# Value, key and query projections with 512 weight columns per matmul instead of 256

## The chip, the cores and the metric

The kernel runs on one core of a Trainium2 chip. The metric is the device time of one execution in microseconds, as a median of three runs. Engines are called as the profile calls them: PE is TensorE (matmuls), PEld its weight loads, DVE is VectorE, ACT is ScalarE, POOL is GpSimd and SP is the queue from which most transfers are issued.

## The reference

One layer of a diffusion backbone for 1024 latent tokens and 256 context tokens, width 1024, in float32. In order: a SwiGLU feed-forward half step (hidden width 2816), a mixer with two branches, and a second SwiGLU half step, each normalized and modulated by values that come from a conditioning vector. The change concerns the mixer, where one projection gives the inputs of both branches:

```
hx = modulate(rms_norm(x, norm2_g), ml[3], ml[4])
hc = modulate(rms_norm(cx, norm2_g), mc[3], mc[4])
bg_l, cg_l, vc_l, q_l, k_l, v_l, gt_l = split(hx @ w_in)      # widths 1024 x3, q 1024, k 256, v 256, 2048
..., k_c, v_c, ... = split(hc @ w_in)
y_conv_l = bg_l * short_conv(cg_l * vc_l, conv_w)
q_l, k_l, v_l = split_heads(q_l, k_l, v_l, q_norm_g, k_norm_g)  # RMS norm of each head of q and k
q_l, k_l = axial rotary of q_l and k_l                          # latent tokens alone
o_l = attention(q_l, [k_c, k_l], [v_c, v_l])                    # 8 query heads, 2 key/value heads of 128
x = x + ml[5] * merge_branches(y_conv_l, o_l, gt_l, ...)
```

Only the latent stream is returned.

## The kernel before

Each float32 operand of a product is split into a high part that a matmul takes exactly (float32r) and a low part, the rest. A product is then three matmuls (`mm3`): high by high, high by low, low by high. Splitting a tensor (`split`) is a cast on ACT for the high part and a subtraction on DVE for the low part.

The kernel goes through these stages: the first feed-forward net, the mixer's wide projections (a form of Strassen's products, the class `Winograd`, object `mix`), then v, k and q, then the convolution's output product, attention, the merge, and the second feed-forward net. Convolution products and attention are interleaved.

**v.** `load_256` fetches 256 columns of `w_in` as two pieces of 1024 elements on each partition (`load_w`: one transfer into a `raw` tile, a high part in a `wh` tile, a low part in a `wl` tile). `proj_256` makes the product for 128 tokens: the tokens' normalized values (`h_hi`, `h_lo`; 8 tiles of 128 rows of the contraction) are the stationary side, 256 weight columns the moving side, 8 x 3 matmuls into half a PSUM bank. The v loop does so for 2 context and 8 latent token tiles; after each, `split` puts the result into v's high and low tiles.

**k and q.** `heads2` is a generator in three steps for two heads and one chunk of tokens (`CC`: 256 context tokens, `C0` and `C1`: 512 latent tokens each). Step one: for each pair of token tiles four times 128 columns into one bank, a copy by ACT (`xb`), four squares with sums by ACT (`hsq`). Step two: eleven small DVE instructions for the reciprocal root (`rsqrt_cols`), a scaling of each head and token tile by DVE, and for latent tokens the rotary: POOL multiplies the swapped halves (`hsw`), DVE the rest, DVE adds. Step three: PE transposes, and the result is copied (q) or split (k). There are 3 such units for k and 8 for q (four pairs of heads by two chunks). The loop at the end of the stage runs a unit's first step, then the last step of the unit before, so that PE has products while DVE works on the former.

**Queues and pools.** The order that is written is not the order on the engines. When the program is built, a planner with its own estimates of durations sets each engine's order: it takes what is ready and stands earliest in the program; `pinned=True` ties an instruction behind the one traced before it on its engine. Tiles of a tag share a fixed number of slots, and a new tile waits until a slot's last reader is done: 3 `raw`, 4 `wh`, 4 `wl` (also used by `mix` and, for `wl`, by the convolution's weights), 38 large tiles of 1024 elements, 11 of 512 elements, 5 PSUM banks for products, 2 for transposes. Transfers of one queue are issued in their planned order.

**Beside the stage.** `late_steps` is the modulation for the second feed-forward net: four halves of 19 steps, 8 of which are a multiply-add of 512 columns on DVE (`macc`). Three steps are run after each v tile, five after each unit of heads. `mix.part_second` splits the first half of `C1`'s normalized values, which `mix` itself needs unsplit. `conv_weights` and `conv_inputs` fetch and split what the convolution product needs.

## Time and profile before

| what | value |
|---|---|
| median of three runs | 2670.65 us (2669.2 to 2675.72) |
| the profiled execution | 2670.08 us |
| its span, first to last instruction | 2668.3 us |
| busy PE, weight loads, DVE, ACT, POOL | 99%, 83%, 75%, 44%, 21% |
| granted TensorE clock | 0.996 |
| first v product to the last q product | 1287.23 to about 1446.3 us |

Line numbers are all L90, because every engine call goes through one helper; instructions are told apart by the tiles that they write and read. In a row such as `ps<-wh,r`, `ps` is a PSUM bank, `wh` a weight tile and `r` the normalized tokens; `h2ch` and `h2cl` are the context tokens' parts. A timeline's row has the start in the span, the length and, behind `x`, how many like instructions were joined; the brackets show how long the engine had sat idle and what it waited for. Matmuls overlap, so a matmul's own length (0.28 us for 256 columns, 0.39 for 512) says little of their pace.

### The profile page before, as it was taken

What the parts mean: (1) busy time and instruction counts of PE and PEld (TensorE: products, weight loads), DVE (VectorE), ACT (ScalarE), POOL (GpSimd) and SP (SyncE); (2) the same over time, 40 slices, a digit from 0 to 9 for tenths busy, and PEclk for the clock granted to TensorE, in tenths of its full rate; (3) what the DMA queues carried; (4) which work ended last, traced back from release to release, by engine and by line L of the source; (5) the groups of instructions that cost most, each with busy time, mean ns of one, the idle gap of its engine ahead of it and who ended that gap; (6) DMA issues with size and microseconds to landing.
All of it is one profiled execution on the core that took longest, in us unless ns stands there. A gap on an engine that the chain in (4) does not pass through costs nothing.

```text
span 2668.3 us, 36840 instructions
## 1 busy us (share of the span) xinstructions
PE 2633.8 (99%) x13373; PEld 2220.0 (83%) x13373; DVE 2002.0 (75%) x3356; ACT 1173.6 (44%) x2317; POOL 558.4 (21%) x449
## 2 busy tenths in 40 slices
PE   8999999999999999999999999999999999999998
PEld 6787799888778878888999888888888888888888
DVE  5788976788887899877598676685458976657885
ACT  6532454333454643333355576574236333334443
POOL 0134301111020034332033122141001532330200
PEclk9999999999999999999999999999999999999999
DMA  8566475345984355342522432113525643227841
GB/s 320 194 194 189 138 230 158 115 131 187 302 206 119 126 179 173 98 134 72 202 68 92 91 95 62 35 41 98 167 87 171 196 146 97 86 88 285 188 90 64
DMA packets 371471, 381.12 MB, mean 143 GB/s; under 512 B 19526, under 2 KB 258264, under 8 KB 371288
## 3 DMA queue, kind: packets, MB, share of 16 engines
q1 hardware_dynamic: 360472, 357.22, 41.4%
q0 software_dynamic: 10816, 21.53, 4.9%
q8 instruction: 105, 1.72, 0.3%
q14 instruction: 78, 0.64, 0.1%
HBM read 308.88 MB, written 69.76 MB: 142 GB/s over the span
## 4 chain that ended last, share of the span: by engine, by line
PE 90%; DVE 5%; DMA 2%; issue 1%; ACT 1%; POOL 1%; SPq 0%; DVEq 0%; POOLq 0%; ACTq 0%
PE ps L90 74%; PE po L90 8%; PE pt L90 8%; DVE wl L90 1%; DVE r L90 1%; DMA raw<-in_ffn_w_in_dram 1%; DVE nt L90 0%; DMA rawm<-in_w_mod_dram 0%; DMA ws<-in_ffn_w_out_dram 0%; DVE u L90 0%; DVE macc L90 0%; POOL s L90 0%; DVE y L90 0%; POOL sum L90 0%; DVE sq_acc L90 0%
## 5 line engine op out<-in xcount | busy, mean ns | idle before, releaser
L90 PE MATMUL ps<-r,wl 128*128 128x512 f32 x5196 | 1206.8, 391 | 9.6 <-DVE wl L90 3.1
L90 PEld LDWEIGHTS ps<-r,wl 128*128 128x128 f32 x5196 | 974.4, 189 | 218.8 <-DVE wl L90 5.9
L90 ACT CAST wl<-raw 128x512 fp32r<-128x512 f32 x287 | 177.7, 620 | 229.8 <-PE ps L90 173.3
L90 DVE TENSOR_TENSOR wl<-raw,wl 128x512 fp32r<-128x512 f32 x287 | 202.3, 706 | 60.6 <-ACT wl L90 56.7
L90 ACT CAST wl<-sum 128x512 fp32r<-128x512 f32 x168 | 103.2, 620 | 231.9 <-PE ps L90 184.9
L90 DVE TENSOR_TENSOR wl<-sum,wl 128x512 fp32r<-128x512 f32 x168 | 152.2, 908 | 17.8 <-ACT wl L90 16.8
L90 POOL TENSOR_TENSOR sum<-raw 128x512 f32<-128x512 f32 x42 | 60.6, 1443 | 497.9 <-DMA raw<-in_w_in_dram 203.2
L90 DVE SCALAR_TENSOR_TENSOR macc<-rawm,silu_c,macc 128x512 f32<-128x512 f32 x178 | 148.0, 849 | 13.5 <-DMA rawm<-in_w_mod_dram 12.8
L90 DVE TENSOR_TENSOR u<-u,ps 128x512 f32<-128x512 f32 x186 | 126.2, 680 | 33.6 <-PE ps L90 33.6
L90 PE MATMUL ps<-wh,r 128*128 128x256 f32 x768 | 141.6, 284 | 0.0
L90 DVE TENSOR_TENSOR pts<-pt,pts 128x512 fp32r<-128x512 f32 x160 | 108.7, 687 | 41.1 <-ACT pts L90 39.3
L90 ACT CAST pts<-pt 128x512 fp32r<-128x512 f32 x160 | 93.3, 595 | 86.4 <-PE pt L90 82.7
L90 DVE TENSOR_REDUCE m<-ps 128x1 f32<-128x512 f32 (+1 forms) x192 | 110.3, 595 | 23.9 <-PE ps L90 22.3
L90 ACT CAST rh<-hid 128x512 fp32r<-128x512 f32 x132 | 81.3, 620 | 104.6 <-PE ps L90 91.6
L90 PE MATMUL ps<-rh,wl 128*128 128x512 f32 x360 | 122.0, 389 | 0.0
L90 PEld LDWEIGHTS ps<-wh,r 128*128 128x128 f32 x768 | 120.8, 192 | 0.7 <-issue 0.6
L90 POOL TENSOR_TENSOR sum<-raw,sum 128x512 f32<-128x512 f32 x42 | 62.0, 1476 | 268.7 <-DVE wl L90 261.8
L90 ACT CAST wh<-raw 128x512 fp32r<-128x512 f32 (+1 forms) x85 | 67.9, 801 | 103.2 <-PE ps L90 70.2
L90 POOL TENSOR_TENSOR s<-raw 128x512 f32<-128x512 f32 x22 | 32.0, 1457 | 378.5 <-DMA raw<-in_ffn_w_in_dram 297.1
L90 PE MATMUL po<-pts,vh 128*128 128x512 f32 x256 | 110.0, 435 | 0.2 <-ACT pts L90 0.2
L90 PE MATMUL ps<-wl,r 128*128 128x256 f32 x384 | 109.0, 284 | 0.0
L90 DVE TENSOR_TENSOR rl<-hid,rh 128x512 fp32r<-128x512 f32 x132 | 90.3, 686 | 21.7 <-PE ps L90 11.7
(317 smaller groups left out, 5382.9 us busy)
## 6 DMA issues: line engine op xcount, KB each, us to landing
raw<-in_ffn_w_in_dram SPq DMA_DIRECT2D x130, 512.0 KB
raw<-in_ffn_w_out_dram SPq DMA_DIRECT2D x72, 512.0 KB
raw<-in_w_in_dram SPq DMA_DIRECT2D x61, 512.0 KB
rawm<-in_w_mod_dram SPq DMA_DIRECT2D x104, 256.0 KB
hid<-hd SPq DMA_DIRECT2D x40, 512.0 KB
rawm<-in_w_mod_dram SPq DMA_DIRECT2D x32, 512.0 KB
ws<-in_ffn_w_out_dram POOLq DMA_DIRECT2D x30, 512.0 KB, 6.5
ucd<-uc SPq DMA_DIRECT2D x29, 512.0 KB
```

The source lines that it names most:

```text
L90: inst = getattr(self.engine, name)(*args, **kw)
```

## The change

One product now makes 512 columns. k and v lie side by side in `w_in`, so k's two heads and v share a product; q is made four heads at a time. `load_512` fetches 512 columns as four pieces, each with 256 rows of the contraction. `tokens2` takes the place of `heads2` and of the v loop, with the same three steps, for two token tiles and `n_h` heads (2 with v, 4 for q): 1 + 4 units for k and v, 2 x 4 for q, 13 in all. Each token tile has a bank of its own; in the last unit of each group (`at_once`) the two banks are filled side by side, piece by piece. `part_second` moves from before v to behind the first unit, nine late steps are run after each unit, the rotary products are written one token tile at a time, and the convolution's first weights are fetched behind the last unit's products instead of before them.

```diff
-    for k in range(4):
-        mix.part_second(k)
...
-    def load_256(o):
+    def load_512(o):
         return [
-            load_w(wi[h * 512 : (h + 1) * 512, o : o + 256].rearrange("(k p) n -> p k n", p=P), (4, 256))
-            for h in range(2)
+            load_w(wi[i * 256 : (i + 1) * 256, o : o + 512].rearrange("(k p) n -> p k n", p=P), (2, 512))
+            for i in range(4)
         ]
...
-    vw = load_256(O_V)
+    kv_w = load_512(O_K)
...
-    for kt in range(10):
-        ch = CC if kt < 2 else C0 if kt < 6 else C1
-        o = (kt if kt < 2 else (kt - 2) % 4) * P
-        pv_ = ps_s(256)
-        proj_256(pv_, vw, ch, o)
-        split(pv_, *v_tile(kt))
-        run(late_steps, 3)
...
+    def tokens2(w, ch, b, n_h, g, dst, values=None, at_once=False):
+        s, o, _ = ch
+        banks, ts = [ps_s(), ps_s()], [(2 * b + t) * P for t in range(2)]
+        terms = [
+            [(*(h(k, ch)[:, at : at + P] for h in (h_hi, h_lo)), *(p[:, k % 2] for p in w[k // 2])) for k in range(KD)]
+            for at in ts
+        ]
+        if at_once:
+            for k in range(KD):
+                for ps, tk in zip(banks, terms):
+                    mm3(ps, tk, k, k + 1)
+        xt, segs, ss = [], [], small("ss", 2 * n_h)
+        for t, (ps, tk) in enumerate(zip(banks, terms)):
+            if not at_once:
+                mm3(ps, tk)
+            if n_h == 4 or t == 0:
+                xt.append(ttile("xb"))
+            seg = xt[t] if n_h == 4 else xt[0][:, t * 256 : (t + 1) * 256]
+            segs.append(seg)
+            act.copy(out=seg, in_=ps[:, : n_h * HD])
+            if values:
+                values(t, ps[:, n_h * HD :])
...
+            xv = seg.rearrange("p (h d) -> p h d", h=n_h)
+            dve.tensor_mul(out=xv, in0=xv, in1=rope_t[0][:, tt][:, None].to_broadcast([P, n_h, HD]))
+        for xb, sb in zip(xt, sw):
+            dve.tensor_add(out=xb, in0=xb, in1=sb)
         yield
+        for h0 in range(0, n_h, 2):
+            pt = ps_t()
+            for e in range(2):
+                for t, seg in enumerate(segs):
+                    at = (2 * e + t) * P
+                    transpose(pt[:, at : at + P], seg[:, (h0 + e) * HD : (h0 + e + 1) * HD], pinned=True)
+                dst(h0 + e, pt[:, e * 256 : (e + 1) * 256])
         yield
...
+        for ch, b in pairs_of:
+            a = ch[1] + b * 256
+            yield tokens2(
+                w, ch, b, 2, 1, lambda h, pt, a=a: split(pt, *(t[:, a : a + 256] for t in k_lat[h])),
+                lambda t, pv, a=a: split(pv, *v_tile(2 + a // P + t)), a == 768,
+            )
+        for i in range(2):
+            w = load_512(O_Q + i * 512)
...
+                yield tokens2(
+                    w, ch, b, 4, 0, lambda h, pt, q4=q4, a=a: act.copy(out=q4[h][:, a : a + 256], in_=pt), None, a == 768
+                )
...
     for i, h in enumerate(heads()):
         run(before, 1)
-        if i == NQ + 2:
+        if i == N_UNITS - 1:
+            conv_inputs(C0)
+        run(h, 1)
+        if i == 0:
+            for k in range(4):
+                mix.part_second(k)
+        if i == N_UNITS - 1:
             conv_weights(0)
             conv_weights(1)
-            conv_inputs(C0)
-        run(h, 1)
         run(before)
-        run(late_steps, 5)
+        run(late_steps, 9)
         before = h
```

More of the change, by code (lines that the diff above doesn't have):

```diff
@@ L1405, in tile_dit_layer @@
         dve.tensor_scalar(out=hg[:, i], in0=pg[:, i * P : (i + 1) * P], scalar1=f, scalar2=None, op0=ALU.mult)
-    def heads2(w, ch, g, dst):
-        s, o, n = ch
-        nt = n // P
-        xt, ss = [], small("ss", 2 * nt)
-        for b in range(nt // 2):
-            ps = ps_s()
-            for t in range(2):
-                proj_256(ps[:, t * 256 : (t + 1) * 256], w, ch, (2 * b + t) * P)
-            xb, sq = ttile("xb"), ttile("hsq")
-            act.copy(out=xb, in_=ps)
-            for i in range(4):
+    def tokens2(w, ch, b, n_h, g, dst, values=None, at_once=False):
[20 more added lines that the diff above has]
+                values(t, ps[:, n_h * HD :])
+            sq = ttile("hsq")
+            for i in range(n_h):
```

77 lines of the change are left out of this document (29 added, 48 removed).

## The prediction

> **What bounds the kernel now.** I read the page first: busy shares, then the chain of work that ended last.
>
> ```profile
> span 2668.3 us, 36840 instructions
> PE 2633.8 (99%) x13373; PEld 2220.0 (83%) x13373; DVE 2002.0 (75%) x3356; ACT 1173.6 (44%) x2317; POOL 558.4 (21%) x449
> PE 90%; DVE 5%; DMA 2%; issue 1%; ACT 1%; POOL 1%; SPq 0%; DVEq 0%; POOLq 0%; ACTq 0%
> ```
>
> PE carries the end, so time can leave only where PE itself issues less or waits less. Each of the 13373 matmuls has its own weight load (PEld, same count). Next, the busy time of the v, k and q stage by stretches, with one stretch of the attention for comparison (columns: stretch, length, PE, PEld, DVE, ACT, POOL, clock, DMA share, GB/s).
>
> ```profile
> 1287.23:1446.70 159.47, 159.47 (x1329) 158.52 (x1328) 125.03 (x318) 71.12 (x237) 36.96 (x72) 1.00 0.35 119
> 1287.23:1316.00 28.77, 28.77 (x240) 28.54 (x239) 15.58 (x27) 6.81 (x14) 0.00 (x0) 1.00 0.67 241
> 1350.00:1446.70 96.70, 96.70 (x809) 96.21 (x809) 87.35 (x233) 49.42 (x170) 32.61 (x64) 1.00 0.27 88
> 1480.00:1520.00 40.00, 39.39 (x209) 32.59 (x209) 25.64 (x55) 23.36 (x57) 7.02 (x5) 1.00 0.54 96
> by line: PE ps L90 94.4%; PE pt L90 5.7%
> ```
>
> The stage takes 159.47 us, PE is busy in all of it, and by the chain cut to 1270 to 1470 us (last line) nothing but PE is on the path. Two things are to be seen. PEld is at 158.52 of 159.47, against 32.59 of 40 in the attention: here the weight loads fill the time, not the streaming of columns. And DVE has room while v is made (15.58 of 28.77) but hardly any in q (87.35 of 96.70, 90%). The Trainium skill (Perfetto Trace Analysis, Identifying the Most-Contended Engine) says that matmul occupancy is a poor measure and weight-load occupancy a good one; by that rule the stretch is bound by loads, and the trace agrees with its 158.52.
>
> **Part 1: half as many matmuls, twice as wide.** The groups by shape give the counts (the mean behind the bar is one matmul's latency, and groups overlap, so pace has to come from elsewhere); the chain and the PE timeline give the pace (start, length, count).
>
> ```profile
> L90 PE MATMUL ps<-wh,r 128*128 128x256 f32 x768 | 141.6, 284 | 0.0
> L90 PE MATMUL ps<-wl,r 128*128 128x256 f32 x384 | 109.0, 284 | 0.0
> L90 PE MATMUL ps<-wh,h2ch 128*128 128x256 f32 x32 | 9.1, 285 | 0.0
> L90 PE MATMUL ps<-wh,h2cl 128*128 128x256 f32 x32 | 9.1, 283 | 0.0
> L90 PE MATMUL pt<-ident,xb 128*128 128x128 f32 x84 | 12.6, 272 | 0.0
> 1399.54 11.40 PE ps L90 x95
> 2204.62 55.70 PE L90 MATMUL ps<-r,wl 128*128 128x512 f32 x245
> 1483.12 3.12 PE L90 MATMUL ps<-y,wc 128*128 128x512 f32 x13
> 1489.77 2.31 PE L90 MATMUL ps<-kl,qs 128*128 128x512 f32 x9
> ```
>
> 256 columns: 768 + 384 for latent tokens and three groups of 32 for context make 1248 matmuls, and 95 of them in 11.40 us are 0.120 us each: 149.8 us. 512 columns: a long undisturbed run gives (55.70 - 0.39) / 244 = 0.2267 (0.39 being one matmul's own latency), the convolution's products beside busy DVE and ACT (3.12 - 0.39) / 12 = 0.2275, the scores (2.31 - 0.39) / 8 = 0.240. After the change there are 624 such matmuls: 141.5, 142.0 or 149.8 us. So the saving lies between 8.3 and 0.0 us. I take 0.2275, since that stream stands nearest in time, surroundings and form (eight products into one bank, other engines reading beside it): **-7.8 us**. It falls wholly on the path, because the stage has no PE gap that it could vanish into. The transposes stay 84 in number (two heads of two tokens for four tokens of one head): nothing.
>
> The Trainium skill (TensorE: Matmul & The Clock Gate, Back-to-back issue gap) states columns / 2.4 + 2.5 ns between isolated matmuls. That is 109.2 and 215.8 ns, an estimate of 2 x 109.2 - 215.8 = 2.6 ns a pair and a sum of only -1.6 us, and it speaks against most of this gain. The rows above say 120 and 227 ns, so here the narrow matmul pays something that its columns don't explain; no run shown measures the wide form with tokens as stationary side.
>
> **Part 2: weights.** A group's weights were two pieces (of 1024 columns on each partition); now they are four, and the pools hold four high parts, four low parts and three raw ones. Before, the next group's two were converted a whole group ahead. Now the next group's quarter j can only be converted once the last unit of this group has read quarter j. The side-by-side order makes that possible during the unit: with 48 matmuls of 0.2275 (10.9 us), quarter 0 is free 2.7 us after its start, the others at 5.5, 8.2 and 10.9.
>
> ```profile
> 1271.15 0.38 SPq L90 DMA_DIRECT2D raw<-in_w_in_dram  x1
> 1275.31 1.05 ACT L90 CAST wh<-raw 128x1024 fp32r<-128x1024 f32 x1 [3.09 <-DMA raw<-in_w_in_dram]
> 1278.34 1.05 ACT L90 CAST wh<-raw 128x1024 fp32r<-128x1024 f32 x1 [0.92 <-DMA raw<-in_w_in_dram]
> 1281.14 1.22 DVE L90 TENSOR_TENSOR wl<-raw,wh 128x1024 fp32r<-128x1024 f32 x1
> 1288.04 1.22 DVE L90 TENSOR_TENSOR wl<-raw,wh 128x1024 fp32r<-128x1024 f32 x1
> 1371.37 0.59 ACT L90 COPY xb<-ps 128x512 f32<-128x512 f32 x1 [0.44 <-PE ps L90]
> 1371.85 1.05 ACT L90 CAST wh<-raw 128x1024 fp32r<-128x1024 f32 x1
> 1372.80 0.31 ACT L90 ACTIVATE hsq<-xb 128x128 f32<-128x128 f32 x1
> 1387.87 3.27 DVE L90 SCALAR_TENSOR_TENSOR xb<-xb,rs_y,hg 128x128 f32<-128x128 f32 x8
> ```
>
> A piece costs 1.05 on ACT and 1.22 on DVE after a transfer of 4.2 (1271.15 to 1275.31). The critical one is quarter 3: free only when the unit ends, and read 18 matmuls (4.1 us) into the next. The rows at 1371 show a cast slipping in behind a copy, ahead of the squares. So: both banks end within 0.7 us of each other, copy, four squares and second copy take about 0.6 + 1.2 + 0.6, from about 0.5 before the unit's end, so the cast starts some 1.9 after it, and the low part is done at 1.9 + 1.05 + 1.22 = 4.2. That is even with the 4.1. Quarters 0 to 2 have 4 us or more of cover. The fourth raw transfer waits until quarter 0's low part is made (2.7 + 1.05 + 1.22 = 5.0 into the unit at best), and lands at 9.2, before its slot is free. A DVE batch of 3.27 in the way is the other end: up to 3.3 a boundary. There are three boundaries (k/v to q, q to q, q to the convolution's weights): 0 to 9.9 us, and I take 0.5 each, **+1.5**, nearer to the low end because the even margin is what the rows give and a batch is in the way only part of the time. At the stage's start four pieces are needed where two were. The trace already makes four there: the last low part ends at 1288.04 + 1.22 = 1289.26, and quarter 3 would be read 4.1 us after 1287.23, at 1291.3: nothing, and if it came 2.1 us later than now, a stall begins.
>
> **Part 3: DVE, ACT, POOL and the queue.**
>
> ```profile
> 1385.64 0.17 DVE L90 TENSOR_SCALAR ssa<-ss 128x8 f32<-128x8 f32 x1 [2.07 <-ACT hsq L90]
> L90 DVE TENSOR_TENSOR xb<-xb,rope x40: 409/413/683, 1345.1 to 1458.8; 128x256 f32<-128x256 f32 x40
> L90 DVE TENSOR_TENSOR xb<-xb,hsw x20: 676/686/836, 1347.0 to 1459.3; 128x512 f32<-128x512 f32 x20
> L90 DVE SCALAR_TENSOR_TENSOR macc<-rawm,silu_c,macc 128x512 f32<-128x512 f32 x28 | 21.3, 761 | 0.3
> L90 DVE TENSOR_TENSOR kl<-pt,kl x4: 678/682/692, 1353.7 to 1367.8; 128x512 fp32r<-128x512 f32 x4
> L90 ACT CAST r<-h x4: 612/618/629, 1243.9 to 1250.6; 128x512 fp32r<-128x512 f32 x4
> L90 DVE TENSOR_TENSOR r<-h,r x4: 678/684/869, 1245.3 to 1251.5; 128x512 fp32r<-128x512 f32 x4
> 1422.97 10.43 SPq L90 DMA_DIRECT2D y<-yd  x8
> 1398.88 0.66 PE pt L90 x6
> ```
>
> Thirteen units instead of eleven run the reciprocal root: from 1385.64 to 1387.87 its eleven small steps take 2.2 us, so +4.4 us of DVE. The rotary products: 40 of 0.413 become 8 of 0.413 and 16 of 512 columns, for which the addition of that width gives 0.686: 16.5 to 14.3 us, -2.2. Four k splits of 0.68 become eight of half the width, at 0.41 by the rotary row: +0.6. So DVE gets about 2.8 us more in a stage 7.8 us shorter: 127.8 of 151.7, 84%, where it was 78%. It isn't the bound on average. In q it is close: a unit is 2.2 + 3.27 + 2 x 0.69 + 2 x 0.69 = 8.2, eight are 65.6; the second group's weights 4.9, two pieces for the convolution 2.4, eight y splits 8 x 0.68 = 5.4, and of the modulation's 28 steps of 0.76 some 13, 9.9: 88 of the 94.4 us that PE takes for eight units (10.9, and eight transposes of 0.66 / 6 = 0.11), 93% after 90%. The modulation's steps move forward (9 a unit where 5 were), into the k/v units, where v formerly left DVE idle. Who waits for a late DVE is PE at a boundary, priced above, and the transposes of the unit before, which have the next unit's 10.9 us as cover: +0.3 for these. POOL (32.61 of 96.70) and ACT (49.42) move the same elements in other widths: off the path.
>
> The split of C1's first half (part_second) moves behind the first unit: 4 x 0.62 on ACT, 4 x 0.68 on DVE. It is first read by the fourth unit, three units (34 us) after the stage's start; without that cover PE would wait 0.62 + 0.68 = 1.3. No queue loses by it: it issues no transfer. On SP the order changes: a fourth raw transfer waits for its slot with transfers of the modulation and y behind it. The y transfers already take 10.43 us to issue while they wait for space. After the change that space (C0's tiles) comes free two units, 22 us, before the convolution reads them: nothing. Work before this stage is unchanged; that after it is planned anew, and of its PE gaps the attention shows 0.61 in 40 us: nothing, with about 2 us either way.
>
> **The sum.** -7.8 + 1.5 + 0.3 = -6.0 us. The profiled execution took 2670.08 us, 1.8 more than its span; 2664.1 there. The median of the three runs, 2670.65, is 0.57 above it, so **2664.6 us**.
>
> **Rivals.** *The whole saving and more* (18%): no boundary stalls, a pace of 0.2267, and up to 2 us of gaps lost later: 2670.65 - 8.3 = 2662.4, down to 2660.3. For it: the even margin of quarter 3, and a PE without gaps today. Against: all three boundaries must hold.
>
> *The pace doesn't come* (6%): the wide form runs as the scores do, at 0.236 to 0.240, so that a pair saves 0 to 4 ns: 0 to 2.5 us, and with the stalls 2670 to 2672. For it, the row at 1489.77; against it, both other rows. The Trainium skill's isolated gap (the same section) gives an estimate of 2670.65 - 1.6 = 2669.1 without stalls.
>
> *DVE eats it* (16%): the saving is there, but with 93% of DVE taken in q, weights and normalized heads come late in several units; 4 to 11 us lost in all: 2667 to 2674. For it, 87.35 of 96.70; against it, that the modulation steps can yield.
>
> *Slower* (10%): the single-buffered weights. If quarter 0's low part is made only behind the 3.27 batch after the unit's end, PE waits 3.3 + 1.2 = 4.5, the fourth raw transfer starts only then, and quarter 3 is there 4.8 + 1.05 + 1.22 = 7.1 later while PE gets to it in 4.1: 3.0 more. 7.5 at each of two boundaries and 4.5 at the convolution are 19.5: 2670.65 - 7.8 + 19.5 = 2682. It decides from 7.8 us of stalls on; for it, that DVE queue; against it, that quarter 0 has 8 us in which to be served.
>
> The forecast holds 50%, from 2662.6 to 2668. About 0.3%, 8 us, can be told from no change here. Faster by more than that is the first rival, 18%; slower is the last, 10%; the rest, 72%, is within. The range 2660 to 2674 leaves out the slow case and the first rival's last tail, some 14%.
>
> **What would show it.** Matmuls and weight loads 12749 each; one group of 512 columns, at 0.227 a start; PEld clearly below PE in the stage, as in the attention; the stage some 6 us shorter. PE waits on a wl or wh of a weight piece at three places, each below 1 us; DVE above 90% in q. A wait of several us of PE on DVE there, or a pace of 0.236, would make me wrong.

## The result and the profile after

The changed kernel takes 2691.89 us (median of six runs, 2688.32 to 2693.51) against 2672.39 for the kernel before in the same session (six runs, 2669.2 to 2675.72): 1.007 times as long, interval 1.0059 to 1.0081. The prediction was 2664.6, within 2660 to 2674. The profiled execution took 2691.47 us.

The page after, its span and its busy shares:

```profile
span 2689.7 us, 35610 instructions
PE 2639.3 (98%) x12749; PEld 2192.3 (82%) x12749; DVE 2002.9 (74%) x3366; ACT 1174.0 (44%) x2342; POOL 554.0 (21%) x417
```

The 624 matmuls fewer are there, and PE was not busy for 50.4 us, where it was 34.5 before. By stretches of the stage (length, PE, weight loads, DVE, ACT, POOL, clock, DMA share, GB/s), and two points of the PE timeline in the first of them:

```profile
1286.40:1403.00 116.60, 116.60 (x528) 95.46 (x527) 76.87 (x201) 43.16 (x147) 16.09 (x24) 1.00 0.37 123
1403.00:1444.60 41.60, 36.76 (x162) 28.37 (x160) 32.16 (x99) 18.13 (x70) 11.26 (x13) 0.96 0.02 5
1444.60:1469.06 24.46, 17.38 (x73) 12.98 (x73) 23.24 (x56) 17.52 (x60) 7.89 (x8) 0.85 0.41 136
1469.06:1479.00 9.94, 7.33 (x18) 4.86 (x18) 9.54 (x17) 2.26 (x3) 3.55 (x4) 0.50 0.45 149
```
```profile
1360.60 0.39 PE L90 MATMUL ps<-wl,r 128*128 128x512 f32 x1
...
1363.35 0.39 PE L90 MATMUL ps<-wl,r 128*128 128x512 f32 x1
```

Until 1403 us PE goes as forecast. Every third matmul is a `wl` one, so the two rows stand twelve matmuls apart: 2.75 / 12 = 0.229 us each. PE has no idle time, and weight loads fill 95.46 of 116.60 where they filled 158.52 of 159.47: they no longer fill the time. When 480 of the 624 products had started, counted from the single records, the changed kernel was 8.3 us ahead; some 1.8 of that are sixteen transposes that it had still to make, at 0.11 us each. Then it loses all of it and more. What stands around 1400 us on DVE, SP, ACT and PE (the brackets show how long the engine had waited, and for what):

```profile
1391.86 2.50 SPq L90 DMA_DIRECT2D rawm<-in_w_mod_dram  x3
1398.49 0.49 DVE L90 TENSOR_SCALAR macc<-rawm,silu_c 128x512 f32<-128x512 f32 x1 [7.08 <-DMA rawm<-in_w_mod_dram]
1406.86 0.62 ACT L90 CAST acch<-macc 128x512 fp32r<-128x512 f32 x1 [9.50 <-DVE macc L90]
1407.38 0.37 ACT L90 COPY q<-pt 128x256 f32<-128x256 f32 x1
1407.80 0.66 PE L90 MATMUL pt<-ident,xb 128*128 128x128 f32 x4 [1.29 <-ACT q L90]
1410.36 0.50 PE L90 MATMUL ps<-wh,r 128*128 128x512 f32 x1 [0.95 <-ACT xb L90]
1428.37 0.16 DVE L90 TENSOR_TENSOR modl<-mcol,bcol 128x4 f32<-128x4 f32 x1 [6.63 <-DMA mcol<-mrow]
```

This is the last of the modulation's four halves. Its rows of `w_mod` were issued late, DVE stood 7.08 us for them, then did its eight steps of the sum by 1406.8, with steps of two units in between, and ACT stood 9.50 us for that sum, with a q copy (1407.38) and the copies out of the product banks queued behind. PE's transposes waited for that q copy and its products for that bank. Nobody stepped aside: an engine's instructions ran in the order that was set when the program was built. At 1428.37 DVE stood another 6.63 us for a column of the modulation. In all it stood 14.2 us at the modulation's transfers in this stage, where in the kernel before it stood 2.2. PE's own waits between 1403 and 1444.6 are 4.8 us. The end of the stage on PE:

```profile
1444.20 0.48 PE L90 MATMUL ps<-wh,r 128*128 128x512 f32 x1
1445.07 0.66 PE L90 MATMUL pt<-ident,xb 128*128 128x128 f32 x4 [0.39 <-ACT q L90]
1446.24 0.44 PE L90 MATMUL pt<-ident,xb 128*128 128x128 f32 x2 [0.52 <-ACT q L90]
1449.60 0.45 PE L90 MATMUL pt<-ident,xb 128*128 128x128 f32 x1 [2.92 <-DVE xb L90]
1450.84 0.48 PE L90 MATMUL pt<-ident,xb 128*128 128x128 f32 x1 [0.79 <-DVE xb L90]
1450.96 3.89 PE L90 MATMUL ps<-y,wc 128*128 128x512 f32 x8
```

Between the last product and the convolution's first, PE goes through transposes of earlier units and waits for them, 6.8 us in all, where before the convolution followed at once. The eight matmuls behind them took 3.89 us, and behind the first scores the clock column says 0.50 for 10 us: after its waits PE runs at half speed for some microseconds. How far DVE was behind is told by the first step of each unit's chain, `ssa<-ss`, which follows the unit's products. The last seven of them, after:

```profile
1377.82 0.16 DVE L90 TENSOR_SCALAR ssa<-ss 128x8 f32<-128x8 f32 x1
1403.83 0.17 DVE L90 TENSOR_SCALAR ssa<-ss 128x8 f32<-128x8 f32 x1
1415.77 0.16 DVE L90 TENSOR_SCALAR ssa<-ss 128x8 f32<-128x8 f32 x1
1430.46 0.16 DVE L90 TENSOR_SCALAR ssa<-ss 128x8 f32<-128x8 f32 x1
1439.63 0.17 DVE L90 TENSOR_SCALAR ssa<-ss 128x8 f32<-128x8 f32 x1
1450.70 0.17 DVE L90 TENSOR_SCALAR ssa<-ss 128x8 f32<-128x8 f32 x1
1464.76 0.16 DVE L90 TENSOR_SCALAR ssa<-ss 128x8 f32<-128x8 f32 x1
```

PE makes a unit in some 11.8 us. Across the modulation's last half there are 26.0 us between two chains; DVE is busy in 15.4 of them and stands in the others. It was behind already: counted from the start of each unit's last product, the chains of the first four units come 1.7 to 2.1 us later, the seventh unit's (1377.82) 12.2 and the eighth's 26.8. The five distances behind the hole average 12.2, with the stand of 6.63 in one and y's eight subtractions in the last, so nothing is made up. PE waits in its turn, and the last chain starts 20.6 us after the last product's start. In the kernel before it starts 2.5 us after it (1448.67).

DVE isn't full in these units, though. From the first q products to the last, columns as above:

```profile
1342.90:1444.60 101.70, 96.86 (x435) 77.45 (x433) 71.99 (x199) 41.80 (x153) 23.81 (x29) 0.98 0.18 55
```

It is busy in 71.99 of 101.70 us, 71%. Much of the rest is spent standing at one instruction while the units' steps stand behind it.

Four landmarks of the two profiled executions add up the difference of 21.4 us (start of the first product, of the last, of the first and the last score against latent keys): before 1287.23, 1446.22, 1458.41 and 1797.63; after 1286.42, 1444.20, 1469.06 and 1814.83. So -0.8 ahead of the stage, -1.2 in the products, **+12.7 from last product to first score**, **+6.6 in the attention**, most of it at its start, and +4.2 behind, of which 3.1 are in the last 60 us. Those 3.1 aren't the change's: kernel 14 below, which has the old products, shows 3.5 there, and kernels 3 and 9, which have the new ones, show nothing.

### The profile page after: what moved, and what is told of

It is laid out like the page before. It is cut to its first block, busy times and chain, and to the rows that moved or that the text cites. A ratio compares the mean times of both kernels' runs of the same rounds, so it can differ in the third digit from the quotient of the medians.

```text
span 2689.7 us, 35610 instructions
## 1 busy us (share of the span) xinstructions
PE 2639.3 (98%) x12749; PEld 2192.3 (82%) x12749; DVE 2002.9 (74%) x3366; ACT 1174.0 (44%) x2342; POOL 554.0 (21%) x417
## 5 line engine op out<-in xcount | busy, mean ns | idle before, releaser
L90 DVE TENSOR_TENSOR wl<-sum,wl 128x512 fp32r<-128x512 f32 x168 | 150.1, 896 | 13.7 <-ACT wl L90 12.7
L90 PE MATMUL ps<-wh,r 128*128 128x512 f32 x384 | 122.6, 397 | 2.5 <-ACT xb L90 2.5
L90 PE MATMUL ps<-kl,qs 128*128 128x512 f32 x384 | 105.1, 398 | 0.0
L90 PE MATMUL ps<-rh,wh 128*128 128x512 f32 x300 | 102.3, 389 | 0.0
```

Source lines behind the costliest of these rows:

```text
L90: inst = getattr(self.engine, name)(*args, **kw)
```

## The experiments

Four lengths tell the kernels apart better than the total time, in which work ahead of the stage varies by some us. All are from start to start in the profiled execution, in us: first to last product ("products"), last product to first score ("to scores"), last product to the first step of the last unit's chain on DVE ("lag"), and first product to last score.

| kernel | median us (runs) | ratio to before, interval | products | to scores | lag | to last score |
|---|---|---|---|---|---|---|
| before | 2672.39 (6) | 1 | 159.0 | 12.2 | 2.5 | 510.4 |
| changed | 2691.89 (6) | 1.007, 1.0059 to 1.0081 | 157.8 | 24.9 | 20.6 | 528.4 |
| 1 late in attention | 2706.61 (4) | 1.0116, 1.0094 to 1.0138 | 149.8 | 13.9 | 6.4 | 542.0 |
| 2 before, same | 2713.15 (4) | 1.014, 1.0119 to 1.016 | 157.2 | 12.2 | 2.5 | 549.8 |
| 3 rawm by POOL | 2691.05 (4) | 1.0058, 1.0038 to 1.0079 | 154.6 | 24.9 | 20.6 | 526.0 |
| 4 conv weights first | 2694.45 (4) | 1.0067, 1.0045 to 1.0089 | 160.4 | 25.3 | 20.6 | 532.0 |
| 5 columns added later | 2687.4 (4) | 1.0052, 1.0034 to 1.0071 | 156.1 | 25.2 | 20.5 | 529.3 |
| 6 less work | 2684.31 (6) | 1.0043, 1.003 to 1.0057 | 151.9 | 25.3 | 20.6 | 524.4 |
| 7 late 16 | 2679.44 (10) | 1.003, 1.002 to 1.0041 | 156.2 | 20.9 | 12.5 | 518.8 |
| 8 late 6 | 2692.34 (4) | 1.0078, 1.0052 to 1.0103 | 150.9 | 34.4 | 29.2 | 530.7 |
| 9 y first | 2688.47 (4) | 1.0064, 1.0049 to 1.0079 | 156.7 | 25.1 | 20.6 | 529.5 |
| 10 y first, as 5 | 2689.06 (4) | 1.0062, 1.0047 to 1.0078 | 156.1 | 25.5 | 20.7 | 528.9 |
| 11 y first, late 16 | 2684.67 (4) | 1.0048, 1.0031 to 1.0065 | 156.2 | 20.9 | 12.5 | 519.0 |
| 12 y first, late 12, as 5 | 2678.03 (10) | 1.002, 1.0011 to 1.0029 | 150.2 | 22.0 | 13.4 | 517.2 |
| 13 late in merge | 2670.73 (11) | 0.9989, 0.998 to 0.9998 | 149.8 | 13.9 | 6.4 | 508.0 |
| 14 before, late in merge | 2675.0 (11) | 1.0002, 0.9993 to 1.0011 | 157.2 | 12.2 | 2.8 | 509.1 |
| 15 as 12, y on POOL | 2679.86 (10) | 1.0022, 1.0013 to 1.0031 | 150.2 | 23.1 | 12.2 | 519.2 |
| 16 before, late in q | 2677.3 (10) | 1.0014, 1.0005 to 1.0023 | 158.5 | 14.8 | 6.3 | 514.6 |
| 17 as 13, weights on POOL | 2670.84 (11) | 0.9994, 0.9985 to 1.0003 | 149.8 | 13.1 | 7.5 | 509.0 |
| 18 as 13, no side by side | 2669.26 (11) | 0.9981, 0.9971 to 0.999 | 149.8 | 12.8 | 6.4 | 504.7 |

### Is it the modulation at all, or the end of the stage's order?

Kernels 1 and 2 are the changed kernel and the one before with the late steps taken out of the stage and run in the attention. The edit of kernel 1 (kernel 2 takes out the calls with 3 and 5 steps):

```diff
-        run(late_steps, 9)
...
-    run(late_steps)
...
             u.scores(len(u.pl))
+            run(late_steps, 2)
             for _ in range(n):
                 run(rest, 1)
...
+    run(late_steps)
```

> The changed kernel, with the modulation's 76 late steps taken out of the k/v/q stage and run two at a time in the attention's units instead; all else as changed. Theory (late data): the loss of some 25 us after 1400 us comes from DVE and ACT standing in order behind the modulation's multiply-adds whose weights landed late (7.1 us on rawm, 6.6 us on mcol, 9.5 us of ACT on macc). Without these steps in the stage PE should stay busy through q, the stage should end 6 to 9 us earlier than in the kernel before, and the total should be 2660 to 2668 us. Rival (load): DVE is simply full in q with 11 us of PE per unit. Then taking 10 us of multiply-adds out of q helps a little, PE still waits on heads and weights at the end of q, and the total stays above 2675. Rival (end order): the convolution's weights and inputs come late because they were moved behind the last unit; then a loss of 8 us or more stays between the last q product and the first scores.

> The kernel before with the same move of the late steps into the attention. It gives the price of the move alone. Late data: the kernel before loses nothing to these steps in its stage (PE gaps there are nil), so 2668 to 2676, no change; the difference to the run above is then the change's own worth, some 7 us. Load: also no change here.

Both lose some 32 to 40 us in the attention, which has no room for the steps, but the stage itself tells what was wanted: without the modulation the products take 149.8 us instead of 157.8, the last chain starts 6.4 us after the last product instead of 20.6, and the first score comes after 13.9 us. The difference of the two totals, -6.5 us, is about the prediction's.

Kernel 3 issues the late rows of `w_mod` from POOL instead of SP; kernel 4 puts the convolution's first two weight tiles ahead of the last unit's products again, as before.

```diff
...
+            if pinned:
+                load(raw[:], src, pinned)
+            else:
+                pool.dma_start(out=raw[:], in_=src)
```
```diff
         if i == N_UNITS - 1:
+            conv_weights(0)
+            conv_weights(1)
             conv_inputs(C0)
         run(h, 1)
...
-        if i == N_UNITS - 1:
-            conv_weights(0)
-            conv_weights(1)
```

> The changed kernel with the late modulation's weight transfers issued from POOL instead of SP, all else as changed. Theory (late data, by the queue): the last four of these transfers stood on SP behind three convolution weights that waited for raw slots until 1391.4, and landed at 1398.5. On a queue of their own they land before DVE needs them: the 7.1 us wait goes to under 1 us, ACT's 9.5 us too, and the total falls to 2665 to 2678. If the transfers were late for lack of space (or the planner places the multiply-adds as early as it can in any case), DVE waits as long as before and the total stays at 2688 to 2694. Load: also 2685 or more.

> The changed kernel with the convolution's first two weights fetched ahead of the last unit's products again, as the kernel before did. End order: the loss after the last q product shrinks and the total falls by 8 us or more, to 2683 or less. Late data: DVE is already 13 us behind by then, so the total moves by less than 4 us, 2686 to 2695.

Neither helps the end. In kernel 3 the products are 3.2 us shorter; the rows are there, and DVE stands for the columns of three halves instead, 4.97 to 5.47 us each. Kernel 4 loses the same at the end. With the rows on another queue the stands only move, from rows to columns.

### Waits, work or place?

Kernel 5 adds to kernel 3 that the four additions of the modulation's columns (`modl<-mcol`) are written behind the stage. Kernel 6 has all transfers and waits, but narrow multiply-adds (it leaves out most of the modulation's sum). Kernels 7 and 8 change the pace, to 16 steps and to 6.

```diff
-                dve.tensor_add(out=mod[:, c0 : c0 + 4], in0=mcol[:], in1=bcol[:, c0 : c0 + 4])
+                if by_four:
+                    adds.append((mod[:, c0 : c0 + 4], mcol[:], bcol[:, c0 : c0 + 4]))
+                else:
+                    dve.tensor_add(out=mod[:, c0 : c0 + 4], in0=mcol[:], in1=bcol[:, c0 : c0 + 4])
...
+    for mod, mc, bc in adds:
+        dve.tensor_add(out=mod, in0=mc, in1=bc)
```
```diff
-                        dve.scalar_tensor_tensor(out=acc, in0=raw, scalar=s, in1=acc, op0=ALU.mult, op1=ALU.add)
+                        n = 64 if by_four else 512
+                        dve.scalar_tensor_tensor(
+                            out=acc[:, :n], in0=raw[:, :n], scalar=s, in1=acc[:, :n], op0=ALU.mult, op1=ALU.add
+                        )
```
```diff
-        run(late_steps, 9)
+        run(late_steps, 16)
```

> The changed kernel with the same late steps at the same pace, but nothing on VectorE waits for a transfer of theirs: the rows of w_mod are fetched from the POOL queue, and the four additions of the modulation's columns are placed behind the stage instead of in it. The VectorE work of the stage is unchanged. Theory 'waits in order' (VectorE stands 5 to 7 us twice on rawm and mcol, ScalarE 7 to 9.5 us on macc, and the units' work stands behind them): the 22 us that are lost between 1400 and 1480 us shrink to under 8, first scores at 1450 to 1458 instead of 1469, time 2668 to 2678. Theory 'too much work' (VectorE is simply full in q): the first scores stay at 1465 to 1470 and the time at 2687 to 2692. Theory 'the units themselves' (the order inside tokens2, whatever the modulation does): as 'too much work', with VectorE idle time elsewhere in the stage.

> The changed kernel with all transfers and waits of the late steps in place, but seven of each eight multiply-adds of the late modulation touch 64 columns instead of 512 (so the second feed-forward net's modulation leaves out most of its sum). That takes about 0.6 us from each of 28 steps, some 17 us of VectorE in all and 8 to 10 of them in q. Theory 'waits in order': VectorE and ScalarE still stand on rawm and mcol, the loss after 1400 us shrinks by less than half, time 2680 to 2690. Theory 'too much work': the loss goes, time 2664 to 2670. Theory 'the units themselves': time 2687 to 2692.

> The changed kernel with 16 late steps behind each unit instead of 9: all 76 are then issued in the first five units (k and v), where VectorE has room, and none in q. Theories 'waits in order' and 'too much work' both expect the loss after 1400 us to go or to move into the k/v units at a smaller size: time 2664 to 2676, first scores at 1449 to 1460. Theory 'the units themselves': no gain, 2687 to 2692. If the loss moves into k/v at full size (first scores still at 1467 or later), then it hangs on the chain of waits and not on the lack of room.

> The changed kernel with 6 late steps behind each unit instead of 9: 19 of the modulation's 28 multiply-adds that stood in q stay there, spread over all eight q units, and the last half's cast, row and column come at the stage's end. Theory 'waits in order': the two stands move from 1398 and 1428 us to the stage's end, and the loss is about as large, 2683 to 2692. Theory 'too much work': VectorE has even more to do in q (about 5 us), so as slow or slower, 2688 to 2697. Theory 'the units themselves': 2687 to 2692.

Kernel 5 doesn't test what it was made for. The planner, which takes what is ready, set the four additions back into the stage, and DVE stands at the columns' transfers for 5.29, 1.08, 4.62 and 5.39 us, 16.4 in all, where the changed kernel stands 14.2. So the waits weren't taken away. Kernel 5 wins 1.7 us in the products and nothing at the end. Kernel 6 has the waits, 16.7 us of them, and little work: it wins 5.9 of the 8 us of the products and nothing at the end, so less work alone isn't enough. Around the modulation's last half, kernel 5, then kernel 6:

```profile
1376.49 0.42 DVE L90 TENSOR_SCALAR ssa<-ss 128x8 f32<-128x8 f32 x1
1393.94 0.16 DVE L90 TENSOR_TENSOR modl<-mcol,bcol 128x4 f32<-128x4 f32 x1 [4.62 <-DMA mcol<-mrow]
1399.12 0.16 DVE L90 TENSOR_SCALAR ssa<-ss 128x8 f32<-128x8 f32 x1
```
```profile
1402.39 0.16 DVE L90 TENSOR_SCALAR ssa<-ss 128x8 f32<-128x8 f32 x1
1420.63 0.16 DVE L90 TENSOR_TENSOR modl<-mcol,bcol 128x4 f32<-128x4 f32 x1 [12.27 <-DMA mcol<-mrow]
1422.71 0.16 DVE L90 TENSOR_SCALAR ssa<-ss 128x8 f32<-128x8 f32 x1
```

Each has a hole of more than 20 us between two chains with a stand for a column in it, and kernel 6 has a second one (24.2 us, with 10.0 of waits for weights and rows). The lag at the end is 20.5 to 20.7 us in seven kernels (changed, 3, 4, 5, 6, 9, 10), though their longest holes differ, 22.6 to 27.2. So it isn't the sum of what was lost; a limit on how far PE's fixed order lets it run ahead would fit, but wasn't tested.

The pace moves the hole. At 6 the last half stands at the stage's end: the products are nearly whole (150.9), the lag is 29.2 and the end the worst of all. At 16 the holes lie in k and v, where the sixth chain comes 27.4 us after its unit's products. DVE stands only 3.9 us at the modulation's transfers in that kernel, so waits for them aren't the whole cause either. From the sixth chain on DVE is at no step of the modulation, and yet it is 12.5 us late at the end, since a unit takes DVE some 9.1 us without any other work and PE 11.8: it gains at most 2.7 us a unit, with weights and y to be fitted in besides. How the loss divides into work, waits for transfers and waits of DVE and ACT for each other stays open.

### What holds up the end?

With 16 late steps, none of the modulation was left in q, and the end still took 20.9. One other thing stood out there: the transfers of `y` went at 1439 (1443.1 in the changed kernel, 1423 before), behind a raw weight tile of the convolution that waits for a slot. Kernels 9 to 12 issue y ahead of it (`conv_raw` issues the transfer of a raw tile alone):

```diff
         if i == N_UNITS - 1:
+            for j in range(3):
+                conv_raw(j)
             conv_inputs(C0)
...
             conv_weights(1)
+            conv_raw(3, True)
```

> The changed kernel with one thing moved on the SP queue: the eight transfers of y go ahead of the fourth transfer of the convolution's raw weights, which waits for a raw slot until the last q unit has read its weights (1442.6 us in the changed kernel, 1438.8 with 16 late steps; before the change y went at 1423 to 1433). Late steps as in the changed kernel. Theory 'two stands' (the modulation's last half costs some 9 us in q up to 1440, and y behind the raw weights costs the rest, some 8 us, between the last q product and the first scores): y issued right after the last column transfer of the modulation, about 1427; stage from last q product to first scores from 24.9 us to 14 to 18; time 2680 to 2686. Theory 'y doesn't matter' (the stage's end is VectorE working off what it lost in q, y's splits only fill in): 2688 to 2692.

> As the run without VectorE's waits for the late steps' transfers (2687.4), with y ahead of the fourth raw transfer besides. Theory 'two stands': the two add up, 2674 to 2682; ScalarE still stands on macc. Theory 'y doesn't matter': 2685 to 2689.

> As the run with 16 late steps behind each unit (2679.4: no late step in q), with y ahead of the fourth raw transfer besides, so that y goes at 1405 to 1420 and its splits are done before the last product. Theory 'two stands': from last q product to first scores 12 to 14 us instead of 20.9, time 2669 to 2674; what is left over the 2666 of the sum are the two waits of PE at 1359 and 1375 us (4.3 us and a halved clock behind the first) which the crowded k and v units cause. Theory 'y doesn't matter': 2677 to 2681.

> All three together at a middle pace: 12 late steps behind each unit (done in the second q unit), w_mod's rows from the POOL queue, the four additions behind the stage, y ahead of the fourth raw transfer. Theory 'two stands': neither the crowd in k and v nor the stands in q, first scores at 1449 to 1453, the sum of the prediction comes out: 2663 to 2669, faster than before. Theory 'y doesn't matter': 2676 to 2684. If the time stays above 2672 though the first scores come before 1453, the rest is lost behind this stage.

The theory of y fell: issued at 1422 (kernel 9) or between 1395 and 1413 (kernel 12), it leaves lag and end as they were. (Kernel 11's total is above kernel 7's though their stages agree: its first product starts at 1294.81 instead of 1285.84, so the difference lies ahead of the stage.) Kernel 12 settles the products: with a middle pace and only 5.7 us of waits for the modulation's transfers, 4.53 of them at the last column, they take 150.2 us with all of the modulation in the stage. Its lag is still 13.4. The end of kernel 12 on PE:

```profile
1436.50 0.39 PE L90 MATMUL ps<-wh,r 128*128 128x512 f32 x1
1436.73 0.60 PE L90 MATMUL pt<-ident,xb 128*128 128x128 f32 x4
1437.58 0.71 PE L90 MATMUL pt<-ident,xb 128*128 128x128 f32 x4 [0.24 <-ACT q L90]
1438.48 0.71 PE L90 MATMUL pt<-ident,xb 128*128 128x128 f32 x4 [0.19 <-ACT q L90]
1439.65 0.44 PE L90 MATMUL pt<-ident,xb 128*128 128x128 f32 x2 [0.46 <-ACT q L90]
1441.07 0.81 PE L90 MATMUL ps<-y,wc 128*128 128x512 f32 x2 [0.98 <-ACT y L90]
1443.53 5.26 PE L90 MATMUL ps<-y,wc 128*128 128x512 f32 x12 [1.65 <-DVE y L90]
```

Fourteen transposes stand ahead of the convolution and wait for the copies that empty their two banks; then the convolution waits for y's halves, which come late like all else, and its twelve matmuls take 5.26 us at a lower clock. By count of the records, 30 of the 84 transposes of the stage are left after the last product here and in the changed kernel, and 22 or 23 of them stand ahead of the first score; in the kernel before 16 are left, and 8 are ahead.

Kernel 15 is kernel 12 with y's low parts taken off DVE: `split(raw, t[:, 0], t[:, 1], lo_eng)`, with `pool` as `lo_eng` for the first chunk of tokens.

> The run with y first, 12 late steps and no wait for transfers (2678.0; first scores 172.2 us after the stage's first product, and VectorE busy 20.96 of the 21.58 us between last product and first scores), with the low parts of the eight y tiles made by GpSimd instead of VectorE, 8 times 0.7 us. Theory 'VectorE has no room': the 21.6 us from last product to first scores shrink by about 5, time 2671 to 2675. Theory 'the stage's end costs of itself': the end stays as long, 2676 to 2680, since the last unit's chain is as long as before.

No gain: the lag shrinks by 1.2 us only, and PE now waited for POOL's halves; the end became 23.1. Its expectation had put about 5 us on the theory that DVE has no room.

### With room on both sides

Kernels 13 and 14 have the late steps taken out of the stage and run in the merge, where DVE was half idle: in the changed kernel and in the one before. What both add:

```diff
             if (j, ch) not in ((0, C0), (1, C0)):
                 run(merge(j, ch))
+                run(late_steps, 6)
+    run(late_steps)
```

> The changed kernel with all late steps taken out of the stage and run in the merge, six behind each of its last 14 products, where VectorE has room (in the trace of before it is busy 44.52 of 90.00 us there). Unlike the run that moved them into the attention, nothing dense is disturbed. Theory 'VectorE has no room in q' (the modulation's last half and the units together don't fit into the shortened stage, whatever their order): the stage keeps its whole saving, first scores 162 to 165 us after its first product (171.2 before, 182.6 after), and with nothing lost later the time is 2662 to 2667, faster than before. Theory 'the stage's end costs of itself' (last q unit's VectorE chain in front of the transposes, with no product to cover it): first scores at 170 or later from its first product, 2670 to 2676.

> The kernel before with the same move of the late steps into the merge. Both theories: its stage has no gap of PE to give back, so it neither wins nor loses there, 2668 to 2673. The difference to the changed kernel with the same move is then what the wide products are worth when VectorE has room: by the sum of the prediction without its stalls 7.8 us, by 'the stage's end costs of itself' 0 to 2 us.

Kernel 13, its products and its end as windows (columns as above), and the end on PE:

```profile
1287.49:1437.40 149.91, 149.91 (x693) 123.30 (x692) 102.36 (x285) 66.31 (x243) 35.92 (x44) 1.00 0.18 54
1437.40:1451.13 13.73, 12.47 (x60) 10.03 (x59) 13.39 (x32) 7.18 (x25) 2.36 (x3) 1.00 0.28 88
```
```profile
1437.26 0.39 PE L90 MATMUL ps<-wh,r 128*128 128x512 f32 x1
1437.49 3.56 PE L90 MATMUL ps<-y,wc 128*128 128x512 f32 x15
1440.89 0.38 PE L90 MATMUL pt<-ident,xb 128*128 128x128 f32 x2
1441.03 2.33 PE L90 MATMUL ps<-y,wc 128*128 128x512 f32 x9
```

PE is busy in all of 149.91 us, and the convolution follows at once, with transposes slipped in by twos. DVE waits for the units now, not they for it:

```profile
1415.89 0.17 DVE L90 TENSOR_SCALAR ssa<-ss 128x8 f32<-128x8 f32 x1 [2.56 <-ACT hsq L90]
1427.77 0.17 DVE L90 TENSOR_SCALAR ssa<-ss 128x8 f32<-128x8 f32 x1 [2.69 <-ACT hsq L90]
1443.69 0.16 DVE L90 TENSOR_SCALAR ssa<-ss 128x8 f32<-128x8 f32 x1
```

So **the loss comes from wide products and late modulation in one stage**: with the modulation moved away, the changed kernel has its products in 149.8 us and its end in 13.9, where it had 157.8 and 24.9. All twelve kernels with a lag over 10 us have both in one stage; none of the eight others has. How late DVE is when the products end goes with how long the end is: in the table lags of 2.5 to 7.5 go with ends of 12.2 to 14.8, lags of 12.2 to 13.4 with 20.9 to 23.1, 20.5 to 20.7 with 24.9 to 25.5, and 29.2 with 34.4.

That the lag alone makes the end long is not shown. The same twelve kernels have 30 or 32 transposes left behind the last product, where the eight others have 16 or 18, so PE's order is a rival. With 30 left, a lag shorter by 7 to 8 us brings an end shorter by 3 to 4 (kernels 7 and 12 against the changed one); the larger step, from 20.9 to 14.8 and less, comes with both at once, and no run separates them.

By its first score, 163.6 us after its first product, kernel 13 bears out the theory that DVE had no room; its time, 2670.7, lies where the other theory had it.

The totals of kernels 13 and 14 differ by 4.3 us, 0.9989 against 1.0002, the products by 157.2 - 149.8 = 7.4. Of these, 1.7 us are given back up to the first score and 4.6 behind it, so that at the last score 1.1 are left (508.0 against 509.1). The spans of the two profiled executions differ by 4.9; the other 3.8 lie ahead of the first product and behind the last score, and nothing shows that they are the change's. In the stretch behind the first score PE waits 1.18 us for the last unit's chain and the clock falls to 0.88:

```profile
1451.10:1465.00 13.90, 12.16 (x49) 9.28 (x48) 10.19 (x17) 5.53 (x11) 1.83 (x2) 0.88 0.46 151
1453.62 0.30 PE L90 MATMUL pt<-ident,xb 128*128 128x128 f32 x1 [1.18 <-DVE xb L90]
```

Kernel 16 asks whether the old units suffer as well when DVE's room in q is taken: the kernel before with no late step in the v loop and seven behind each unit.

```diff
-        run(late_steps, 3)
...
-        run(late_steps, 5)
+        run(late_steps, 7)
```

> The kernel before, products untouched, but no late step while v is made and 7 instead of 5 behind each unit of k and q, which moves 30 of the 76 late steps (about 12 of the 28 multiply-adds, 9 us of VectorE) out of the v loop into a stretch where VectorE is already busy 90%. Theory 'VectorE has no room': the kernel before loses as the changed one did, PE waits on xb and q appear in a stage that had none, 2676 to 2686. If it stays at 2668 to 2673, then a full VectorE alone doesn't stop PE, and the changed kernel's units must be more sensitive than the old ones.

It loses a little, 0.14%: the lag is 6.3 instead of 2.5 and the end 2.6 us longer, but its products are as fast as ever (158.5), and DVE stands at none of the modulation's transfers. So the old units are far less sensitive; that their longer products (157.2 us against 149.8) leave DVE the time to catch up fits, but wasn't tested by itself.

### Two details, and the fastest version

Kernel 17 makes the low parts of the convolution's second and third weight tile on POOL (`conv_weights(1, pool)`, `conv_weights(2, pool)`); kernel 18 fills the two banks of a group's last unit one after the other (`at_once` false everywhere). Both stand on kernel 13.

> The run with the late steps in the merge (2670.7; between its last product at 1437 us and the attention's start PE loses 5.4 us more than before, with VectorE busy 13.46 of 13.80 us), and besides the low parts of the convolution's second and third weight tile made by GpSimd instead of VectorE, 2.4 us in the chain that VectorE works off there. Theory 'the stage's end hangs on VectorE's last chain' (y's splits, weight tiles and the last unit's steps, one behind the other): first scores and the first attention unit come 1.5 to 3 us earlier, 2667 to 2670. Theory 'it hangs on the order of PE' (transposes of the last unit put ahead of scores): unchanged, 2670 to 2672. GpSimd needs longer for such a tile than VectorE; if PE then waits on wc, it is slower, 2672 to 2676.

> The run with the late steps in the merge, with the two banks of a group's last unit filled one after the other, as in all other units, instead of side by side. By the working of the prediction's second part a quarter of the weights is then free not at 2.7, 5.5, 8.2 and 10.9 us of the unit but at 6.8, 8.2, 9.5 and 10.9; the fourth raw transfer starts 4.1 us later, and the last quarter's low part is there some 0.6 us after PE wants it: 0 to 2 us at each of two boundaries, 2671 to 2675. If nothing is lost (2669 to 2672), the margin at the boundaries is larger than I had worked out; if 4 us or more, the side-by-side order carries the change.

Kernel 17 is kernel 13 again within its noise: the end is 0.8 us shorter, and the attention gives that and 1.0 more back. Its expectation had named this, an unchanged time, for the theory that the end hangs on PE's order. Kernel 18 has the lowest time of all, 0.9981 (0.9971 to 0.999) of the kernel before, though its interval overlaps that of kernel 13. Its stage as windows, the second row up to the first score:

```profile
1290.17:1440.25 150.08, 150.08 (x694) 123.29 (x693) 101.84 (x285) 65.44 (x247) 33.78 (x44) 1.00 0.17 54
1440.25:1452.77 12.52, 12.52 (x61) 10.15 (x60) 12.14 (x31) 6.99 (x21) 2.54 (x3) 1.00 0.33 106
```

PE is busy throughout, so the weights' boundaries cost nothing even without the order that was made for them. To the last score it takes 504.7 us, 4.4 less than the kernel before with the same move (kernel 14).

## Why the prediction was wrong, step by step

- **Part 1, the products: right.** -7.8 was predicted; with the modulation out of the way on both sides it is -7.4. Kernel 13's window has 624 wide and 69 narrow matmuls in 149.91 us; with 0.11 for a narrow one that is 0.228 each, where I took 0.2275. The low end, at which the wide form runs as the scores do, is out, and so is the sum by the Trainium skill's isolated gap (TensorE: Matmul & The Clock Gate, Back-to-back issue gap): it gave an estimate of -1.6.
- **Part 2, the weights: too dear, harmless.** +1.5 was predicted for three boundaries, up to 9.9. No run's PE waited on a weight piece at the two boundaries into q. The rival *Slower* came out in sign only; its mechanism is nowhere in the trace.
- **Part 3, DVE, is the step that failed**, in two sentences. Late normalized heads and transposes were priced at +0.3, since "the transposes of the unit before, which have the next unit's 10.9 us as cover", and the rival *DVE eats it* says that "the modulation steps can yield". They can't: a multiply-add that stands ahead of a unit's step on DVE runs ahead of it, and so does a cast on ACT, even while it waits for a transfer. And the lateness adds up. I had counted DVE's work against the time, 93% in q; the trace shows 71% (71.99 of 101.70). What the count left out are the stands, 14.2 us at the modulation's transfers alone. They and the work threw the chain back to 26.8 us behind its unit's products. A unit without other work wins back 2.7 us at most (9.1 on DVE, where I had summed 8.2, against 11.8 on PE), so nine units would be needed to come back to the 2.4 of an undisturbed one, and five come after. In place of +0.3 stand up to 7.6 us in the products (157.8 against 150.2 in kernel 12) and 9 to 13 at the end, with some of the 6.6 in the attention. *DVE eats it* had the right engine, a cause that was only in part right (lack of time, not standing in order) and too small a size: 4 to 11 us lost, some 27 measured (19.5 by the medians and the 7.4 that the products saved).
- **The last unit has no cover.** The next unit's 10.9 us, which carried the +0.3, don't exist behind the last product. The third boundary was priced for weights and not for transposes.
- **SP, "nothing": the price stands, its reason doesn't.** y was not there 22 us early but went at 1443.1, 1.1 us ahead of the last product's start; bringing it forward returned nothing that can be measured (kernel 9).
- **"Nothing, with about 2 us either way" for the attention:** it took 6.6 us more from first to last score, and even with the modulation away 5.1 (kernel 13) and 2.9 (kernel 18).

What stays open: why that stretch is longer in kernels 13 and 18, beyond the 2 or 3 us of waits and clock shown behind the first score. Open too is whether the end hangs on DVE's lateness or on PE's order. And a stage in which DVE waits for none of the modulation's transfers, or the last half spread evenly over several units, wasn't tried.

## What to carry to other kernels

A saving on the bounding engine is worth what the engines beside it can follow, and a busy share doesn't tell that: ask how far the follower is thrown back by the longest piece of side work and by what that piece waits for, and how many rounds it needs to make that up with what is left over in each. Follow one step of its chain through the rounds (here `ssa<-ss`) and compare it with the end of the products. Where an experiment is to take a wait away, look in its trace whether the wait is gone: in kernel 5 it wasn't. Where side work was laid into a stage's holes and the stage is then shortened, move the side work to a place with room: with that, and the banks filled in turn, 0.7% of loss became 0.2% of gain.

## What the runs showed of the hardware

After waits of a few microseconds PE can run at half clock for some 3.6 us. In the changed kernel these rows follow the one of 1410.36 above, ahead of which PE had waited 1.29, 0.52 and 0.95 us:

```profile
1411.06 1.05 PE L90 MATMUL ps<-wh,r 128*128 128x512 f32 x2
1412.34 1.05 PE L90 MATMUL ps<-wh,r 128*128 128x512 f32 x2
1413.62 0.88 PE L90 MATMUL ps<-wh,r 128*128 128x512 f32 x2
1414.58 0.62 PE L90 MATMUL ps<-wh,r 128*128 128x512 f32 x2
```

Three matmuls take 1.28 us from 1411.06 to 1412.34, 0.427 each, and full speed is back after 1414. So waits of 2.8 us in sum cost another 1.7 or so. In kernel 7 one wait was enough:

```profile
1362.22 0.47 PE L90 MATMUL ps<-wh,r 128*128 128x512 f32 x1 [2.40 <-DVE vl L90]
```

From 1363.4 to 1367.0 the granted clock is 0.53 there, and before the wait and from 1367 on it is 1.00. The Trainium skill (TensorE: Matmul & The Clock Gate, Part 1: The HAM clock gate) says that the clock goes to half after an idle window of about 3.4 us and back after a busy one of that length. The way back agrees, some 3.6 us in both. The way down differs in kernel 7, where PE sat idle for 2.40 us and not 3.4. In the changed kernel it can't be told, since there the last product ends 3.85 us ahead of 1410.36 and only transposes stand between. Not every stretch of this length does it: in kernel 3 one of 2.34 us without a product, with transposes in it, was followed by full speed, so these runs give no threshold.
